# The second half of the differential values moved ahead of the products with the inverse, and score steps put in the places it leaves

## Chip, core and metric

The kernel runs on one core of a Trainium2 chip. The metric is the device time of one execution in microseconds (us). A core has a tensor engine (PE, with PEld for its weight loads), a vector engine (DVE), a scalar engine (ACT), GpSimd (POOL) and SyncE (SP), which here only issues transfers. Each engine works through its own list of instructions in order, and an instruction that waits holds up those behind it on its engine.

## What is computed

Two transformer blocks over 512 tokens of width 1024. The change is in the attention of the second block, which has two independent halves whose outputs are joined and multiplied by one output matrix:

```
# half 1: RWKV-7, 8 heads of 64, a recurrence over the tokens
sa = einsum('bhvk,bhk->bhv', state, -kk_t)
state = state * w_t + sa * (kk_t * a_t) + v_t * k_t
y_t = einsum('bhvk,bhk->bhv', state, r_t)
...
# half 2: differential attention, 4 heads, two score maps each
pr = softmax(where(dist >= 0, q k^T * scale - slopes * dist, NEG_INF))
attn = pr[:, :, 0] - lam * pr[:, :, 1]
out = einsum('bhqk,bhkv->bhqv', attn, vh)
```

The recurrence is done in 8 chunks of 64 tokens. Inside a chunk a triangular system has to be inverted. Products of fp32 values are made of three fp32r matmuls, from a value's high part and its rest (`whi`, `wlo` for weights, `xh`, `xl` for activations).

## The kernel before

All that follows is in `block2_attn`. First come the projections. For a weight chunk, a transfer brings `raw`, ACT casts it to `whi` (L168), and DVE or POOL subtracts to get `wlo` (L169). There are two buffers each of `whi` and `wlo`.

`inverse32` (L1642) inverts the diagonal 32x32 blocks on DVE alone, in a long chain of multiplies and sums, and ends with two transposes, `tN` (L1673) and `tT` (L1674). While it runs, PE does the last projections: the queries and keys of the differential half (`diff_qk`, tile `psd`), and its values (`diff_v`, L1288, tile `psdv`). `diff_v(0)` gives the first half of the values, `diff_v(1)`, called `values1`, the second half. Each is 96 matmuls over two weight chunks, whose `wlo` POOL makes. One step of `values1` is 12 matmuls.

Then the 64x64 inverses are put together. `psi` (L1443) multiplies `tN` with the blocks below the diagonal, in 32x32 matmuls; its result is copied to `pm`, half by DVE and half by ACT. A second product, also called `psi` (L1449), gives the corner, which is copied into `TT` (L1450). `chunk_in(0)` opens the bank `pxy` of chunk 0 (L1388, a product with the all-zero tile `zero`, and L1390). DVE copies it to `xs`, PE applies the inverse (`pu`, L1470), and the result `uv` goes into the new state (`pst`, L1480, tile `S`). The loop over the 8 chunks follows, each with `pxy`, `xs`, `pu`, `uv` and `pst` of its own.

The tile `zero` is written by POOL (L1352) into the space (tag `zq`) of `Qb`, a work tile of `inverse32`.

`diff_heads` is a generator, called `work`, of the softmax steps. A score step (16 of them, h a head, b a query block, of 128, 256, 384 or 512 keys) makes two products `z` on PE (L656), for each a sum with `dist` and a minimum on DVE (L657) and an exponential on ACT (L659), then on DVE a reciprocal (L662), a small product (L1722) and the difference of the two maps (L1723). A turned step transposes it (`t`, L675) and copies it to `w` (L677). A weighted step multiplies by the values (`o`, L683). Steps come in the order score 0, score 1, score 2, turned 0, score 3, turned 1, weighted 0, and so on.

The order on PE is written out by hand. `fill(n, of)` puts the next n steps of a generator at its place. `VF = (3, 2, 2, 2)` are the counts of the places before the loop and in chunk 0, `FILLS = (2, 2, 1, 6, 6, 0, 0)` those of the later chunks and of `tail`, which also puts all that is left. `rest()` runs what is left of `values1` and makes the tiles that take over the space of the activations `xh`: the states `S`, the second distance tile, and `yr`. DVE, ACT and POOL instructions are put in order by a scheduler.

Of the kernel before, what the change touches and what calls it, by code (L numbers as in the profile page):

```python
# [82 lines left out]
class Net:  # L83
# [999 lines left out]
    def block2_attn(self):  # L1083
        nc, A = self.nc, self.A
        v_, g_, s_, t_ = nc.vector, nc.gpsimd, nc.scalar, nc.tensor
        with ExitStack() as st:
# [192 lines left out]
            def diff_v(half):  # L1279
                pss = [p_.tile([128, 2, 256], F32, tag=n_, name="psdv") for p_, n_ in ((pz, "s"), (ptp, "t"))]  # L1280
                for c in range(2):
                    hi, lo = self.chunk(A["w_dv"][2 * half + c], g_)
                    for j in range(4):
                        k, cc = 4 * c + j, slice(j * 256, j * 256 + 256)
                        for t in range(4):
                            o, tb = pss[t // 2][:, t % 2, :], slice(t * 128, t * 128 + 128)
                            for i, (a, b) in enumerate(((xh, hi), (xh, lo), (xl, hi))):
                                t_.matmul(o, a[k][:, tb], b[:, cc], start=k == 0 and i == 0 and t % 2 == 0,  # L1288
                                          stop=k == 7 and i == 2, skip_group_check=True)
                        if k < 7:  # L1290
                            yield
                for t in range(4):
                    s_.activation(out=dv[:, t, half * 256:half * 256 + 256], in_=pss[t // 2][:, t % 2, :], func=AF.Copy, scale=rc[:, t:t + 1])
# [51 lines left out]
            values1 = diff_v(1)  # L1345
# [13 lines left out]
            def rest():  # L1359
                for _ in values1:  # L1360
                    pass
                dist2[1] = self.xp.tile([128, S], F32, tag="xh2", name="dist2")
                yr.extend(self.xp.tile([128, S], F32, tag=f"xh{4 + t}", name=f"yr{t}") for t in range(4))
                for i in range(2):
                    S2.append(self.xp.tile([128, 4, 2, 64], F32, tag=f"xh{i}", name=f"S{i}"))
                    g_.memset(S2[i], 0.0)
# [13 lines left out]
            fill = lambda n, of=work: [next(of, None) for _ in range(n)]  # L1380
            banks = {}

            def chunk_in(c):
                cp, par = c // 2, c % 2
                U, V = E[1 - par], E[par]
                p_, n_ = ((pr, "r"), (py, "y"))[c % 2]
                b = banks[c] = p_.tile([128, 512], F32, tag=n_, name="pxy")
                t_.matmul(b, zero[:, 0:128], zero, start=True, stop=False, skip_group_check=True)  # L1388
                for h in range(8):
                    t_.matmul(b[U, hs[h]], lm(par, cp, h)[V, 64 - 64 * par:128 - 64 * par], vt[V, cp, hs[h]], start=False, stop=True, skip_group_check=True)  # L1390
                s_.copy(out=uv2[V, c % 2, :], in_=vt[V, cp, :])
# [30 lines left out]
            with self.tc.manual_schedule(engines={mybir.EngineType.PE}):  # L1422

                TT = [pp.tile([128, 4, 2, 64], F32, tag=n_, name="TT") for n_ in ("pb0", "pb1", "e20", "e21")]
                pm = pp.tile([128, 4, 8, 32], F32, tag="bk2", name="pm")
                half = [(64 - 64 * par, slice(64 - 64 * par, 96 - 64 * par), slice(96 - 64 * par, 128 - 64 * par)) for par in range(2)]
                for t in range(4):
                    for _, lo, hi in half:
                        g_.memset(TT[t][hi, :, :, 0:32], 0.0)
                        v_.tensor_copy(out=TT[t][lo, :, :, 0:32], in_=tT[lo, :, 2 * t:2 * t + 2, :])  # L1430
                        s_.copy(out=TT[t][hi, :, :, 32:64], in_=tT[hi, :, 2 * t:2 * t + 2, :])

                def corner(ps, hh, rows, mm, out):
                    for par in range(2):
                        for cp in range(4):
                            for h in range(4):
                                mm(ps[half[par][rows], cp, h, :], par, cp, 4 * hh + h)
                    for par in range(2):
                        out(par, ps[half[par][rows]])

                for hh in range(2):
                    ps = ((pg, pv)[hh]).tile([128, 4, 4, 32], F32, tag="go"[hh], name="psi")
                    corner(ps, hh, 2, lambda o, par, cp, h: t_.matmul(o, lm(par, cp, h)[half[par][1], half[par][0] + 32:half[par][0] + 64],  # L1443
                                                                      tN[half[par][1], cp, h, :], start=True, stop=True),
                           lambda par, p: (s_.copy if par else v_.tensor_copy)(out=pm[half[par][2], :, 4 * hh:4 * hh + 4, :], in_=p))
                fill(VF[0], values1)
                for hh in range(2):
                    ps = pc.tile([128, 4, 4, 32], F32, tag="c", name="psi2")
                    corner(ps, hh, 1, lambda o, par, cp, h: t_.matmul(o, pm[half[par][2], cp, h, :], tT[half[par][2], cp, h, :], start=True, stop=True),  # L1449
                           lambda par, p: [(s_.copy if par else v_.tensor_copy)(out=TT[2 * hh + i][half[par][1], :, :, 32:64], in_=p[:, :, 2 * i:2 * i + 2, :])  # L1450
                                           for i in range(2)])
                chunk_in(0)
                fill(VF[1], values1)
                for c in range(8):
                    cp, par = c // 2, c % 2
                    U = E[1 - par]
                    b, uv, xs = banks[c], uv2[:, c % 2, :], xs2[:, c % 2, :]
                    if c:
                        for t in range(4):
                            t_.matmul(b[:, t * 128:t * 128 + 128], ar[t][:, c, :], S2[c % 2][:, t].rearrange("p e v -> p (e v)"),  # L1460
                                      start=False, stop=True, skip_group_check=True)
                    v_.tensor_copy(out=xs[U, 0:256], in_=b[U, 0:256])
                    v_.tensor_copy(out=xs[U, 256:512], in_=b[U, 256:512])
                    if c:
                        chunk_out(c - 1)
                    fill(FILLS[0]) if c else fill(VF[2], values1)
                    for g in range(2):
                        pu = pc.tile([128, 256], F32, tag="c", name="pu")
                        for h in range(4 * g, 4 * g + 4):
                            t_.matmul(pu[U, hs[h - 4 * g]], TT[h // 2][U, cp, h % 2, :], xs[U, hs[h]], start=True, stop=True)  # L1470
                        (s_.copy if g else v_.tensor_copy)(out=uv[U, 256 * g:256 * g + 256], in_=pu[U])
                    if c:
                        fill(FILLS[1])
                    else:
                        rest()
                        fill(VF[3])
                    if c < 7:
                        ps = pc.tile([128, 4, 64], F32, tag="c", name="pst")
                        for h in range(8):
                            t_.matmul(ps[E[h % 2], h // 2, :], bkt[:, c, hs[h]], uv[:, hs[h]], start=True, stop=True)  # L1480
                        for e in range(2):
                            new = S2[(c + 1) % 2][E[e], :, e, :]
                            if c == 0:
                                v_.tensor_copy(out=new, in_=ps[E[e]])
                            else:
                                old = S2[c % 2][E[e], :, e, :]
                                g_.tensor_tensor(out=new, in0=old, in1=dcs[E[e], :, c:c + 1].to_broadcast([64, 4, 64]), op=ALU.mult)
                                v_.tensor_tensor(out=new, in0=new, in1=ps[E[e]], op=ALU.add)
                    if c < 7:
                        chunk_in(c + 1)  # L1490
                    fill(FILLS[2])
                    if c in (4, 6):
                        norm_out(c // 2 - 2)
                if TAIL[0] == 0:
                    tail()
# [320 lines left out]
FILLS = (0, 2, 2, 4, 6)  # L1816
# [177 lines left out]
VF = (3, 2, 2, 2)  # L1994
# [18 lines left out]
FILLS = (2, 2, 1, 6, 6, 0, 0)  # L2013
# [33 lines left out]
```

## Time and profile before

| | us |
|---|---|
| median of 3 runs | 2049.07 (2044.24 to 2054.25) |
| profiled execution | 2044.56 |
| its span | 2042.8 |
| PE busy | 1931.4 |
| DVE busy | 1349.0 |
| ACT busy | 896.6 |
| POOL busy | 428.5 |

The profile describes one execution. Its span runs from the first to the last instruction; 1.76 us lie around it. The granted clock is the share of full speed that the tensor engine had: 1.00 is 2.4 GHz and 0.50 is 1.2 GHz. The stage that the change touches lies between 1470 and 1606 us of the span.

### The profile page before, as it was taken

What the parts mean: (1) busy time and instruction counts of PE and PEld (TensorE: products, weight loads), DVE (VectorE), ACT (ScalarE), POOL (GpSimd) and SP (SyncE); (2) the same over time, 40 slices, a digit from 0 to 9 for tenths busy, and PEclk for the clock granted to TensorE, in tenths of its full rate; (3) what the DMA queues carried; (4) which work ended last, traced back from release to release, by engine and by line L of the source; (5) the groups of instructions that cost most, each with busy time, mean ns of one, the idle gap of its engine ahead of it and who ended that gap; (6) DMA issues with size and microseconds to landing.
All of it is one profiled execution on the core that took longest, in us unless ns stands there. A gap on an engine that the chain in (4) does not pass through costs nothing. (4 is left out here: it accounts for less than half of the span.)

```text
span 2042.8 us, 29679 instructions
## 1 busy us (share of the span) xinstructions
PE 1931.4 (95%) x11652; PEld 1645.2 (81%) x11652; DVE 1349.0 (66%) x2286; ACT 896.6 (44%) x1538; POOL 428.5 (21%) x429
## 2 busy tenths in 40 slices
PE   9959998999999999988899999879989999999997
PEld 7736687999997877778899998768778788888886
DVE  6525668867777666557867676777858668666324
ACT  5425544434344455535434344534246545444321
POOL 2324310000001165420000001355333242111001
PEclk9979999999999999999999999889989999999998
DMA  4230042424222210114423232222210113322332
GB/s 160 70 69 20 28 143 77 133 75 136 70 93 91 85 43 27 35 55 145 142 75 111 86 106 61 97 88 68 73 53 27 66 57 102 100 96 93 94 94 70
DMA packets 57987, 169.38 MB, mean 83 GB/s; under 512 B 6288, under 2 KB 13368, under 8 KB 57848
## 3 DMA queue, kind: packets, MB, share of 16 engines
q1 hardware_dynamic: 54544, 162.51, 24.1%
q10 hardware_dynamic: 3224, 4.72, 1.2%
q8 instruction: 91, 1.49, 0.3%
q14 instruction: 48, 0.39, 0.1%
q0 software_dynamic: 80, 0.26, 0.0%
HBM read 161.70 MB, written 5.77 MB: 82 GB/s over the span
## 5 line engine op out<-in xcount | busy, mean ns | idle before, releaser
L168 ACT CAST whi<-raw 128x1024 fp32r<-128x1024 f32 (+3 forms) x146 | 144.4, 990 | 285.0 <-PE o L175 93.5
L169 DVE TENSOR_TENSOR wlo<-raw,whi 128x1024 fp32r<-128x1024 f32 (+3 forms) x138 | 163.9, 1188 | 127.3 <-ACT whi L168 126.8
L710 PE MATMUL pa<-t,h 128*128 128x256 f32 x960 | 177.3, 286 | 10.3 <-DVE u L884 8.4
L1018 POOL TENSOR_TENSOR acc<-acc,sqt 128x256 f32<-128x256 f32 (+1 forms) x58 | 70.5, 1215 | 487.7 <-ACT sqt L1017 485.8
L207 DVE TENSOR_TENSOR l<-r,h 128x1024 fp32r<-128x1024 f32 x104 | 127.0, 1221 | 53.8 <-ACT h L206 53.8
L710 PEld LDWEIGHTS pa<-t,h 128*128 128x128 f32 x960 | 152.1, 193 | 12.7 <-ACT ah L835 8.7
L710 PE MATMUL pa<-t,l 128*128 128x256 f32 x480 | 137.4, 286 | 1.9 <-DVE l L207 1.9
L206 ACT CAST h<-r 128x1024 fp32r<-128x1024 f32 x104 | 107.7, 1046 | 66.8 <-PE pd L175 20.6
L175 PE MATMUL o<-xl,whi 128*128 128x512 f32 (+1 forms) x352 | 134.6, 383 | 1.6 <-DVE xl L214 1.6
L174 PE MATMUL o<-xh,whi 128*128 128x512 f32 (+1 forms) x352 | 134.8, 383 | 0.0
L176 PE MATMUL o<-xh,wlo 128*128 128x512 f32 (+1 forms) x352 | 134.0, 381 | 0.0
L176 PE MATMUL pd<-ah,l 128*128 128x512 f32 x320 | 126.8, 396 | 2.0 <-DVE l L207 2.0
L174 PE MATMUL pd<-ah,h 128*128 128x512 f32 x320 | 126.7, 396 | 0.3 <-ACT h L206 0.3
L175 PE MATMUL pd<-al,h 128*128 128x512 f32 x320 | 126.6, 396 | 0.0
L710 PE MATMUL p<-t,h 128*128 128x256 f32 x640 | 117.8, 284 | 4.1 <-ACT h L206 4.1
L710 PE MATMUL pb<-t,h 128*128 128x256 f32 x640 | 115.9, 282 | 0.0
L710 PEld LDWEIGHTS p<-t,h 128*128 128x128 f32 x640 | 100.5, 191 | 6.0 <-ACT h L206 4.5
L710 PEld LDWEIGHTS pb<-t,h 128*128 128x128 f32 x640 | 99.8, 191 | 1.0
L206 ACT CAST h<-raw 128x768 fp32r<-128x768 f32 (+2 forms) x76 | 62.3, 820 | 84.9 <-PE pd L175 60.8
L710 PEld LDWEIGHTS pa<-t,l 128*128 128x128 f32 x480 | 93.0, 194 | 2.7 <-DVE l L207 2.7
L710 PE MATMUL p<-t,l 128*128 128x256 f32 x320 | 91.0, 284 | 3.0 <-DVE l L207 3.0
L710 PE MATMUL pb<-t,l 128*128 128x256 f32 x320 | 90.4, 283 | 1.1 <-DVE l L207 1.1
(548 smaller groups left out, 5337.1 us busy)
## 6 DMA issues: line engine op xcount, KB each, us to landing
r<-w_gu SPq DMA_DIRECT2D x88, 512.0 KB, 3.5
raw<-w_gu SPq DMA_DIRECT2D x56, 512.0 KB, 3.5
raw<-w_dn SPq DMA_DIRECT2D x48, 384.0 KB, 4.0
raw<-w_in SPq DMA_DIRECT2D x22, 512.0 KB, 3.5
raw<-w_dn SPq DMA_DIRECT2D x16, 448.0 KB, 3.2
raw<-w_qka SPq DMA_DIRECT2D x8, 512.0 KB, 3.7
raw<-w_dn SPq DMA_DIRECT2D x16, 256.0 KB, 2.6
raw<-w_out SPq DMA_DIRECT2D x8, 512.0 KB, 3.5
```

The lines of the kernel that those rows point to most:

```text
L168: nc.scalar.copy(out=hi[:, :n], in_=raw[:, :n])
L169: (eng or nc.vector).tensor_sub(out=lo[:, :n], in0=raw[:, :n], in1=f(hi[:, :n]))
L174: mm(out, lh, rh, start=start, stop=False)
L175: mm(out, lh, rl, start=False, stop=False)
L176: return mm(out, ll, rh, start=False, stop=stop)
L206: self.nc.scalar.copy(out=hi, in_=src)
L207: (eng or self.nc.vector).tensor_sub(out=lo, in0=src, in1=f(hi))
L710: self.nc.tensor.matmul(c, l, r, start=first and n == 0, stop=k == 3 and n == 2, skip_group_check=True)
L1018: return nc.gpsimd.tensor_add(out=self.acc[:, c], in0=self.acc[:, c], in1=t)
```

## The change

All of `values1` runs before `psi`, by a call of `rest()` there. The four fills that took steps of `values1` take steps of `work` now, three, two, two and two of them: score 0, 1 and 2 behind the first `psi`, turned 0 and score 3 behind `chunk_in(0)`, turned 1 and weighted 0 behind the copies to `xs`, score 4 and turned 2 behind `pu`. So nine steps of `work` less are left for the later places.

```diff
@@ -1438,19 +1438,20 @@
+                rest()
                 for hh in range(2):
                     ps = ((pg, pv)[hh]).tile([128, 4, 4, 32], F32, tag="go"[hh], name="psi")
...
-                fill(VF[0], values1)
+                fill(VF[0])
                 for hh in range(2):
                     ps = pc.tile([128, 4, 4, 32], F32, tag="c", name="psi2")
...
                 chunk_in(0)
-                fill(VF[1], values1)
+                fill(VF[1])
                 for c in range(8):
...
-                    fill(FILLS[0]) if c else fill(VF[2], values1)
+                    fill(FILLS[0]) if c else fill(VF[2])
...
                     if c:
                         fill(FILLS[1])
                     else:
-                        rest()
                         fill(VF[3])
```

On PE, before the change, 18 of the `psi` products stand between two products of the first half of the values; names are tiles, and `x18` counts equal neighbours.

```order
L1288 MATMUL psdv<-whi,xl_12090 128x256
L1288 MATMUL psdv<-whi,xh_12083 128x256
L1443 MATMUL psi<-tN,lms 32x32 x18
L1288 MATMUL psdv<-wlo,xh_12083 128x256
L1288 MATMUL psdv<-whi,xl_12091 128x256
```

After the change all 192 `psdv` stand ahead of `psi`, and PE has this behind the last of them, up to `pu` of chunk 0.

```order
L1288 MATMUL psdv<-whi,xl_12094 128x256
L1444 MATMUL psi<-tN,lms 32x32 x64
L656 MATMUL z<-dqk_13196,dqk_13197 128x128 x2
L656 MATMUL z<-dqk_13196,dqk_13197 128x256 x2
L656 MATMUL z<-dqk_13196,dqk_13197 128x384 x2
L1450 MATMUL psi_13993<-tT,pm 32x32 x32
L1450 MATMUL psi_14030<-tT,pm 32x32 x32
L1388 MATMUL pxy<-zero 128x512
L1390 MATMUL pxy<-vt,lms 64x64 x8
L675 MATMUL t<-ident,s 128x128
L656 MATMUL z<-dqk_13196,dqk_13197 128x512 x2
L675 MATMUL t<-ident,s 128x128 x2
```

The `psi` products are in one piece, and the places between them and `pu`, which held 36 and 48 `psdv`, hold scores and transposes; one `o` follows, then `pu`.

On DVE, after the change, the copies of the corner to `TT` and of the chunk to `xs` have the steps of scores 0 to 2 ahead of them; this is the end of those steps.

```order
L662 RECIPROCAL smst<-smst 128x1
L1722 SCALAR_TENSOR_TENSOR smst<-smst,c_12157,dsum 128x1
L657 ISA s,smst<-z,dist 128x384
L657 ISA smst 128x1
L1723 SCALAR_TENSOR_TENSOR s<-s,smst 128x256
L657 ISA s,smst<-z,dist 128x384
L657 ISA smst 128x1
L662 RECIPROCAL smst<-smst 128x1
L1722 SCALAR_TENSOR_TENSOR smst<-smst,c_12157,dsum 128x1
L1723 SCALAR_TENSOR_TENSOR s<-s,smst 128x384
L1451 COPY TT<-psi_13993 32x8x32 x2
L1451 COPY TT<-psi_14030 32x8x32 x2
```

Before, nothing stood between the copies to `pm` and those to `TT` on DVE.

On POOL, `zero` keeps its place after the change: ahead of the `wlo` of the second chunk of `diff_v(0)` (the first of `x2`) and of both chunks of `diff_v(1)`.

```order
L169 TENSOR_TENSOR wlo<-raw,whi 128x1024 x5
L1352 TENSOR_SCALAR zero<-ident 128x512
L169 TENSOR_TENSOR wlo<-raw,whi 128x1024 x2
L1366 MEMSET S_13873 128x512
L169 TENSOR_TENSOR wlo<-raw,whi 128x1024
L1366 MEMSET S_13875 128x512
```

Before, the three `wlo` behind `zero` stood together; now the clearing of a state stands ahead of the last.

## Rows read from the trace of the kernel before

**Rows 1.** The page: busy time of each engine, its share of the span, instructions.

```profile
PE 1931.4 (95%) x11652; PEld 1645.2 (81%) x11652; DVE 1349.0 (66%) x2286; ACT 896.6 (44%) x1538; POOL 428.5 (21%) x429
```

**Rows 2.** Busy time by stretch: length, then each engine, clock, DMA share, GB/s.

```profile
1519.77:1580.53 60.76, 59.25 (x648) 47.66 (x647) 53.45 (x190) 35.71 (x95) 22.12 (x24) 1.00 0.05 19
1580.53:1606.26 25.73, 23.20 (x150) 18.22 (x151) 21.85 (x91) 15.55 (x37) 5.66 (x4) 0.93 0.30 104
```

**Rows 3.** The chain that ended last, 1486 to 1518: start, length, work.

```profile
1486.32 1.94 PE psi L1443 x36
1488.25 6.97 PE psdv L1288 x47
...
1498.05 4.50 PE psdv L1288 x36
1502.55 3.86 PE psi L1449 x128
...
1507.91 7.44 PE psdv L1288 x48
1515.35 1.07 PE pu L1470 x16
1516.42 1.63 PE psdv L1288 x12
```

**Rows 4.** PE in order of time; in brackets the idle time before and its releaser.

```profile
1486.32 1.94 PE L1443 MATMUL psi<-tN,lms 32*32 32x32 f32 x36 [9.92 <-DVE tN L1673]
```

**Rows 5.** POOL in order of time, 1482 to 1495.

```profile
1482.65 1.49 POOL L1352 TENSOR_SCALAR zero<-ident 128x512 fp32r<-128x512 f32 x1 [13.76 <-DVE Pb L1668]
1484.11 2.37 POOL L169 TENSOR_TENSOR wlo<-raw,whi 128x1024 fp32r<-128x1024 f32 x1
1492.59 2.40 POOL L169 TENSOR_TENSOR wlo<-raw,whi 128x1024 fp32r<-128x1024 f32 x1 [6.12 <-ACT whi L168]
```

**Rows 6.** Stretches by granted clock, columns as in rows 2.

```profile
948.40:951.70 3.30, 3.30 (x18) 3.30 (x18) 2.62 (x4) 1.35 (x4) 0.00 (x0) 0.52 0.02 5
...
1486.30:1490.90 4.60, 4.58 (x49) 4.52 (x50) 4.06 (x9) 2.69 (x7) 0.17 (x1) 0.51 0.36 114
...
1507.95:1511.40 3.45, 3.45 (x17) 3.45 (x18) 0.77 (x2) 0.57 (x1) 0.66 (x1) 0.51 0.00 0
```

**Rows 7.** PE in order of time in the feed-forward part, as in rows 4.

```profile
946.51 0.50 PE L710 MATMUL p<-t,h 128*128 128x256 f32 x2 [2.07 <-ACT h L206]
947.77 0.39 PE L710 MATMUL p<-t,l 128*128 128x256 f32 x1 [0.76 <-DVE l L207]
```

**Rows 8.** DVE in order of time: copies of `psi`, a weight's rest.

```profile
1498.09 0.70 DVE L1445 COPY pm<-psi 32x512 f32<-32x512 f32 x1 [1.13 <-PE psi L1443]
...
1506.45 0.76 DVE L1450 COPY TT<-psi 32x256 f32<-32x256 f32 x2 [1.07 <-PE psi L1449]
...
1511.90 1.22 DVE L169 TENSOR_TENSOR wlo<-raw,whi 128x1024 fp32r<-128x1024 f32 x1 [3.19 <-ACT whi L168]
```

**Rows 9.** Score steps by source line: ns least/median/most, first and last start, forms.

```profile
L657 DVE CUSTOM_DVE_ANT_0 s<-z,dist x32: 278/486/691, 1518.5 to 1589.0; 128x128 f32<-128x128 f32 x8, 128x256 f32<-128x256 f32 x8, 128x384 f32<-128x384 f32 x8, 128x512 f32<-128x512 f32 x8
...
L659 ACT ACTIVATE s<-s,smst x32: 385/556/724, 1519.8 to 1589.7; 128x128 f32<-128x128 f32 x8, 128x256 f32<-128x256 f32 x8, 128x384 f32<-128x384 f32 x8, 128x512 f32<-128x512 f32 x8
L659 ACT ACTIVATION_READ_ACCUMULATOR s<-s,smst x32: 184/187/210, 1520.1 to 1590.4; 128x1 f32 x32
```

**Rows 10.** DVE groups by form, 1520 to 1606: count, busy us, mean ns, idle before.

```profile
L1722 DVE SCALAR_TENSOR_TENSOR smst<-smst,c,dsum 128x1 f32<-128x1 f32 x16 | 5.0, 319 | 0.2
...
L1723 DVE SCALAR_TENSOR_TENSOR s<-s,smst 128x384 f32<-128x384 f32 x4 | 3.6, 890 | 0.1
...
L662 DVE RECIPROCAL smst<-smst 128x1 f32<-128x1 f32 x16 | 2.4, 158 | 0.7 <-ACT s L659 0.5
```

**Rows 11.** PE in order of time: scores of 128 and of 512 keys.

```profile
1530.61 0.49 PE L656 MATMUL z<-dqk,dqk 64*128 64x128 f32 x4
...
1544.63 1.13 PE L656 MATMUL z<-dqk,dqk 64*128 64x512 f32 x4
```

## Prediction

> **What bounds the kernel now.** I read the page first. PE is busy for 95% of the span, DVE for 66% [rows 1], so time is mostly to be had where PE waits, or where it runs at half clock. Then the chain that ended last, in the stage of the change: from 1486.32 to 1518.05 us it is PE without a gap, `psi` and `psdv` in turns, up to `pu` and twelve more `psdv` [rows 3]. So here PE's work sets the pace, and the `psdv` stand where PE would otherwise wait for copies. Then PE in order of time: just ahead of this, it waits 9.92 us, put down to `tN` on DVE [rows 4]. Then POOL: `zero` waits 13.76 us for the last use of `Qb` in the inversion, ends at 1484.14, and the `wlo` behind it runs until 1486.48 [rows 5]. The `psdv` that PE wants next read this `wlo`. So two things end that wait at nearly the same time, `tN` and `wlo`. Last the windows: the 60.76 us of the loop hold 59.25 of PE at full clock and 53.45 of DVE; the 25.73 us behind it hold 23.20 of PE at a granted clock of 0.93, and DVE is busy for 21.85 [rows 2]. PE and DVE are both nearly full there.
>
> **The change, part by part.** The profiled execution took 2044.56 us, 4.5 us (0.2%) below the median of the three runs; I add up against the former and shift to the latter.
>
> *The long wait stays.* The moved `psdv` stand behind the ones that wait for `wlo`, and on POOL this `wlo` is still behind `zero`. PE starts at 1486.48 instead of 1486.32: +0.2. That nothing is gained here rests on the order alone, which the front shows for POOL.
>
> *The values in one piece.* At 1486.48, 47 `psdv` of the first half are left. PE ran at half clock from 1486.30 to 1490.90 [rows 6]. At the full-clock rate of 4.50 us for 36, 0.125 us each [rows 3], it does about 18 of the 47 until 1490.9 and the other 29 by 1494.5. The next chunk's `wlo` ends at 1494.99 [rows 5]; the 92 `psi` covered this before, now PE waits: +0.5 to +1, I take +0.7. The 96 `psdv` took 4.50 + 7.44 + 1.63 = 13.57 us before [rows 3], as part of the 48 ran at half clock (1507.95 to 1511.40 [rows 6]). In one piece at 0.125 they take 12.0: -1.6.
>
> *From `psi` to `pu`.* Before, 1515.35 - 1498.05 = 17.30 us, of which 11.94 are `psdv` (36 and 48): 5.36 us of other PE work [rows 3]. Now this and four scores: 0.49 us of PE for 128 keys and 1.13 for 512 [rows 11], on a line between them 0.70 and 0.92, plus some 0.7 for the transposes and `o`: 9.3 us. But DVE has a chain to do in this order. From the end of `psi`: the copy to `pm` 0.70 and a `wlo` of 1.22 [rows 8] end at 1.9. Score 0: two reads of `z` at 0.28 and the second exponential of 0.39 + 0.19 [rows 9], reciprocal and product 0.16 + 0.32 [rows 10]: 3.5. Score 1, with reads of 0.42 and an exponential of 0.50 + 0.19 (on a line between least and most): 5.5. Score 2 with 0.55 and 0.61 + 0.19: 7.9. The differences L1723, 0.89 for 384 keys [rows 10] and in proportion 0.3 and 0.6: 9.7. Only then come the copies to `TT`, 2 x 0.76 [rows 8]: 11.2; `xs` and `w` add about 1.2: 12.4. On PE the third score waits for the reads of the second (4.7), ends at 5.2, and the second `psi` (3.86), `pxy` (1.50, from 1506.41 to 1507.91), `t`, `z` and `o` (1.8) end at 12.4 too [rows 3]. So `pu` comes 12.4 us behind `psi`, with 9.3 of work: +3.1 of waiting. Bounds: 0 if the reads come sooner (ACT and DVE overlap more), 5 if each hand-over costs more than these rows show.
>
> *The clock in that stretch.* The trace has no such stretch, so I take bounds. In the feed-forward part PE waited 2.07 and 0.76 us within 2 us [rows 7], and ran at a granted 0.52 from 948.40 to 951.70 [rows 6]: 1.2 GHz. Here it waits 3.1 us within 5, after 3.9 us of 32x32 products; and before the change the clock fell at 1507.95 after 32x32 products with no wait at all [rows 3, 6]. So I take it that the clock falls. At half clock 36 `psi` took 1.94, at full 128 took 3.86 [rows 3]: a factor of 1.8. The second `psi` then costs 6.9 instead of 3.86, `pxy` 2.7 instead of 1.5, the last `z`, `t` and `o` 3.2 instead of 1.8: +5.6, of which some overlaps the start of the fall. I take +5. The lower bound is 0: in the loop, waits of 60.76 - 59.25 = 1.5 us in all left the clock at 1.00 [rows 2].
>
> The Trainium skill, page "TensorE: Matmul & The Clock Gate", section "A second HAM failure mode: psum-queue depth-cycling", tells of a kernel whose PE paused briefly between groups of matmuls while it cycled through PSUM banks, and whose clock swung between its two levels. Here `z` has two banks that DVE must read before the next score. By that page the term is +5, by the loop's row 0; rows 6 and 7 side with the page.
>
> *Behind `pu`.* Nine steps fewer are left behind. The loop's places hold as many steps as before, and its PE and DVE are as full, so I expect its length unchanged. Behind the loop, PE waited 2.5 us, and a clock of 0.93 over 25.73 us means 3.6 at half speed, worth 1.8 [rows 2]: 4.3 us at most. DVE has less to do there now, but the last chunk's norm, over DVE, ACT and POOL, still follows `chunk_out(7)`. I take half: -2, between 0 and -4.3.
>
> Sum: 0.2 + 0.7 - 1.6 + 3.1 + 5.0 - 2.0 = +5.4 us. That is 2050.0 for the profiled execution, and 2054.5 beside the median of 2049.07 (+0.26%).
>
> **The rivals.** *The clock holds* (0 instead of +5): 2049.5. For it speaks the loop at 1.00; against it rows 6 and 7. *The values fill the long wait.* If `wlo` came sooner, 9.92 us would go, and with them the half clock up to 1490.90, worth 2.3: 5.4 - 12.2 = -6.8, or 2042.3, faster by 0.3%. Against it stands POOL's order. *The clock stays down into the loop*, the one that makes it clearly slower: a chunk of the loop is 60.76 / 7 = 8.7 us, nearly all PE; at 1.8 times as long it costs up to 6.6 more each. One chunk gives 2061, two give 2068. It decides from 0.7 of a chunk on, where the total passes +10. Each half-clock stretch of rows 6 ended within 5 us, under dense products; these are smaller. *The tail takes it all back*, with the clock held: 5.4 - 5 - 2.3 = -1.9, or 2047.2.
>
> **How the numbers follow.** Forecast 0.60; clock holds 0.18; tail takes it back 0.05; values fill the wait 0.04; clock down into the loop 0.13. A difference of 0.5%, 10.2 us, is about what a measurement of this kernel can tell from no change. Only the slow rival passes it, with a little of the forecast's upper end: slower 0.15. Faster by 10 us would need the filled wait and the tail together: 0.03. The rest, 0.82, is within. The range leaves out the filled wait and the second chunk at half clock: 2045 to 2062.
>
> **What would show it.** Right: PE idle for about 10 us up to 1486.5, then 143 `psdv` with a wait of some 0.7 us at 1494 to 1495; `psi` ending near 1511; three waits of `z` on DVE; the copies to `TT` over 8 us behind `psi`; a granted clock of 0.50 during the second `psi`; `pu` some 18 us behind the first. Wrong: `psdv` running between 1477 and 1486; or a granted 1.00 between `psi` and `pu`; or a tail shorter by more than 4 us, where I have under-rated what DVE's lighter end is worth; or 0.50 beyond the state of chunk 1.

## The result, and the profile after

The changed kernel takes 2060.84 us (median of 7 executions, 2057.96 to 2064.84), the kernel before 2049.07 (2041.79 to 2054.25): a ratio of 1.0065, interval 1.0047 to 1.0083. It is slower by 0.65%; the forecast was +0.26%. The profiled execution of the changed kernel took 2062.12 us, 17.6 more than that of before, so the two profiles overstate the difference of the medians (11.8) by some 6 us.

PE's line of the page after, which answers to [rows 1], shows PE busy for 13.5 us more with the same 11652 products:

```profile
PE 1944.9 (94%) x11652; PEld 1655.5 (80%) x11652; DVE 1349.6 (66%) x2286; ACT 897.4 (44%) x1538; POOL 426.0 (21%) x429
```

So the products are slower, not more. Where, the windows tell. First the stage from the last normalisation ahead of the inverse to the first `psg`, a product behind the loop and its tail, of before:

```profile
1411.50:1601.60 190.10, 176.11 (x1573) 149.45 (x1572) 145.07 (x382) 81.48 (x181) 66.01 (x58) 0.96 0.17 56
```

And the same stage after, followed by `psi` to `pu`, the stretch at half clock, the loop and the tail (the last two answer to [rows 2]), and a second stretch at half clock inside the loop:

```profile
1412.40:1620.70 208.30, 190.96 (x1587) 160.05 (x1586) 150.38 (x398) 83.00 (x182) 65.11 (x58) 0.89 0.16 52
1511.43:1530.20 18.77, 16.50 (x167) 11.83 (x167) 9.90 (x32) 5.54 (x18) 2.04 (x2) 0.52 0.09 29
1512.65:1539.70 27.05, 25.59 (x229) 19.76 (x230) 13.54 (x48) 8.00 (x27) 4.76 (x5) 0.50 0.07 21
1533.65:1602.48 68.83, 66.95 (x665) 54.86 (x665) 51.55 (x197) 35.18 (x89) 20.60 (x23) 0.91 0.03 11
1556.84:1563.50 6.66, 6.66 (x39) 6.08 (x39) 3.61 (x21) 2.08 (x6) 0.86 (x1) 0.50 0.01 2
1602.48:1624.20 21.72, 19.25 (x125) 14.89 (x124) 18.84 (x65) 11.60 (x25) 4.91 (x4) 0.92 0.34 117
```

The stage is 18.2 us longer. PE's idle time in it goes from 14.0 (190.10 - 176.11) to 17.3 us: +3.3. The other 14.9 are PE busy for longer, at a granted clock of 0.89 instead of 0.96. Not all of that is the clock: the window after holds 14 products more (1587 for 1573), which before come behind its end. With the same products, over the whole execution, it is the 13.5 us of the page. A clock of 0.50 is 1.2 GHz, 1.00 is 2.4, so the means stand for about 15 us at half clock before (2 x 0.04 x 190) and 46 after (2 x 0.11 x 208). The 31 more would cost at most about 15, if every product took twice as long. One stretch of 27.05 us holds most of them, and it runs on through `pu` into chunk 1; the loop, at 1.00 before, is at 0.91.

POOL in order of time after, which answers to [rows 5], and below it PE, which answers to [rows 4]; the brackets name idle time and releaser:

```profile
1483.50 1.49 POOL L1352 TENSOR_SCALAR zero<-ident 128x512 fp32r<-128x512 f32 x1 [13.77 <-DVE Pb L1668]
1484.95 2.36 POOL L169 TENSOR_TENSOR wlo<-raw,whi 128x1024 fp32r<-128x1024 f32 x1
1493.46 2.39 POOL L169 TENSOR_TENSOR wlo<-raw,whi 128x1024 fp32r<-128x1024 f32 x1 [6.14 <-ACT whi L168]
```

```profile
1487.37 0.58 PE L1288 MATMUL psdv<-wlo,xh 128*128 128x256 f32 x1 [10.13 <-POOL wlo L169]
...
1495.90 0.39 PE L1288 MATMUL psdv<-wlo,xh 128*128 128x256 f32 x1 [0.58 <-POOL wlo L169]
...
1507.49 3.93 PE L1444 MATMUL psi<-tN,lms 32*32 32x32 f32 x128
1511.35 0.49 PE L656 MATMUL z<-dqk,dqk 64*128 64x128 f32 x4
1513.80 1.43 PE L656 MATMUL z<-dqk,dqk 64*128 64x256 f32 x4 [1.96 <-DVE smst L657]
1515.54 2.25 PE L656 MATMUL z<-dqk,dqk 64*128 64x384 f32 x4 [0.32 <-DVE smst L657]
1517.72 6.47 PE L1450 MATMUL psi<-tT,pm 32*32 32x32 f32 x128
...
1530.20 0.58 PE L1471 MATMUL pu<-xs,TT 64*64 64x64 f32 x3
```

The long wait is still there, 10.13 us, now put down to `wlo`. Behind the first `psi` PE waits twice for DVE, 2.28 us together. The clock fell in the first of these waits (a granted 0.62 from 1511.84 to 1513.80); the second `psi`, 4 us behind the wait, takes 6.47 us where the first takes 3.93. From 1515.54 to `pu` PE does not wait again. It is DVE that waits for PE there, before both copies to `TT`:

```profile
1521.18 0.76 DVE L1451 COPY TT<-psi 32x256 f32<-32x256 f32 x2 [0.62 <-PE psi L1450]
1524.23 0.76 DVE L1451 COPY TT<-psi 32x256 f32<-32x256 f32 x2 [2.28 <-PE psi L1450]
```

### The profile page after: what moved, and what is told of

The parts are those of the page before. It is cut to its first block, busy times and chain, and to the rows that moved or that the text cites. A ratio compares the mean times of both kernels' runs of the same rounds, so it can differ in the third digit from the quotient of the medians.

```text
span 2060.4 us, 29680 instructions
## 1 busy us (share of the span) xinstructions
PE 1944.9 (94%) x11652; PEld 1655.5 (80%) x11652; DVE 1349.6 (66%) x2286; ACT 897.4 (44%) x1538; POOL 426.0 (21%) x429
```

## The experiments

Three questions. Is the loss the clock (theory 1) or the waits between `psi` and `pu` (theory 2)? What keeps the values out of the long wait (theory 3)? And can both be had? Dense products are here the `psdv` and the added ones, weights of 128x128 against 256 or 512 columns. Each kernel was timed in turns with the kernel before on one chip; the ratios are to that.

### Dense products behind `psi`, and no scores behind `psi`

Two kernels that part theory 1 from 2. The first adds eight products whose result nobody reads (`vt` by the identity):

```diff
+                def warm(n, p_, n_):
+                    b = p_.tile([128, 512], F32, tag=n_, name="warm")
+                    for _ in range(n):
+                        t_.matmul(b, self.ident, vt[:, 0, :], start=True, stop=True)
...
                 for hh in range(2):
+                    if hh:
+                        warm(2, pr, "r")
                     ps = ((pg, pv)[hh]).tile(... name="psi")
...
-                fill(VF[0])
+                for n in (2, 1, 1):
+                    fill(1)
+                    warm(n, pr, "r")
                 for hh in range(2):
+                    if hh:
+                        warm(2, pr, "r")
                     ps = pc.tile(... name="psi2")
```

> The changed kernel with eight dense products added (vt by the identity, 128x512, result not read): two between the halves of psi, two behind score step z128, one each behind z256 and z384, two between the halves of psi2. They cost about 0.9 us each at the full clock, some 7 us together, of which 2 to 3 us may lie in PE's own waits (1.96 us ahead of z256, 0.32 ahead of z384). Theory 1 (the loss is the granted clock: about 46 us at half clock between the inverse and the first out product, against 13 before): the half clock behind psi goes or shrinks to under 10 us, 8 to 13 us come back, 5 are paid: 2050 to 2055 us. Theory 2 (the loss is the order and the waits of DVE and ACT between psi and pu, clock aside): the dummies only add, 2064 to 2068 us.

The second takes the three score steps between `psi` and `psi2` away; they follow later:

```diff
-VF = (3, 2, 2, 2)
+VF = (0, 2, 2, 2)
```

> The changed kernel with no score step between psi and psi2 (the three go to the later places). Theory 2 (waits): DVE and ACT come to the copies of pm and TT about 3 us sooner, pu starts 3 to 5 us sooner behind psi, and 3 us or more come back: 2056 to 2058 us. Theory 1 (clock): psi, psi2 and the 64x64 products stand back to back with still less dense work among them, the clock falls to 0.5 behind psi as in the changed kernel and stays down into chunk 1; pu may start sooner, but what is gained is under 2 us: 2059 to 2063 us.

With the dummies 2053.11 us, ratio 1.0024 (1.0012 to 1.0035); without the scores 2059.41, ratio 1.0059 (1.0044 to 1.0075), which is not told apart from the changed kernel. The windows of the kernel with dummies: its stage, `psi` and what follows, then the 27.05 us that were at 0.50, then the loop.

```profile
1411.40:1612.00 200.60, 185.83 (x1604) 152.45 (x1603) 150.47 (x398) 82.76 (x182) 65.17 (x58) 0.96 0.17 54
1506.48:1525.00 18.52, 18.52 (x289) 11.88 (x289) 8.57 (x28) 7.01 (x20) 0.40 (x1) 1.00 0.09 30
1512.65:1539.70 27.05, 27.00 (x313) 18.11 (x311) 17.22 (x61) 11.38 (x36) 4.77 (x5) 1.00 0.03 11
1525.50:1600.00 74.50, 72.56 (x766) 58.66 (x765) 62.32 (x227) 43.13 (x110) 25.46 (x28) 1.00 0.10 30
```

The windows of the kernel without the scores: `psi` and the start of `psi2`, then the stretch at half clock.

```profile
1506.00:1512.60 6.60, 6.60 (x202) 6.47 (x201) 2.62 (x3) 3.49 (x7) 0.00 (x0) 0.91 0.02 6
...
1511.30:1536.00 24.70, 23.93 (x206) 17.97 (x202) 13.34 (x42) 7.54 (x23) 4.73 (x5) 0.52 0.07 23
```

Eight products, about 0.99 us each, were added, and the kernel became 7.7 us faster than the changed one (8.4 by the two ratios, since the kernel before varied between the series): the clock stays at 1.00 from `psi` to the end of the loop, and from the first `psi` product to `pu` it takes less time with the dummies (1506.5 to 1527.8, 21.3 us) than without (1507.5 to 1530.2, 22.7). Without scores the clock falls all the same, at 1511.30, while PE is busy for the whole 6.60 us of the window. In the changed kernel the fall lay in a wait, which the dummies fill too; but here no wait is needed for it. From 1506.44 until the clock falls PE does the 32x32 products of `psi` and `psi2`, with nothing dense beside them. Theory 1 holds. Theory 2 expected 2064 to 2068 and 2056 to 2058.

### Part of the values back behind `psi`

This undoes a part of the change: 36 of the 96 products return to their place of before. They stand there instead of the three score steps, which follow later as in the run without scores.

```diff
-                rest()
+                fill(5, values1)
                 for hh in range(2):
                     ps = ((pg, pv)[hh]).tile(... name="psi")
...
-                fill(VF[0])
+                rest()
```

> The changed kernel with 36 of the 96 products back between psi and psi2, in place of the three score steps there (which go later); 60 stay in front of psi. Theory 1 (what is missing behind psi is dense work): the clock stays full through psi2 and falls later or for a shorter time, 2051 to 2057. Theory 2 (it is the score steps in the waits, on DVE and ACT): with none of them between psi and psi2 it gains what the run without them there gained, 1 to 2 us, 2058 to 2060.

It takes 2053.89 us, ratio 1.0038 (1.0025 to 1.0051). Its windows: from `psi` to `psi2`, then the half clock.

```profile
1500.56:1513.00 12.44, 12.44 (x294) 12.19 (x293) 4.32 (x6) 4.28 (x9) 0.00 (x0) 1.00 0.15 46
1513.00:1527.00 14.00, 13.22 (x70) 7.99 (x69) 8.12 (x32) 5.67 (x18) 2.04 (x2) 0.51 0.13 39
```

With 36 `psdv` between them both `psi` run at 1.00; the clock falls behind the second, where the changed kernel has small products too, and for 14 us instead of 27. This is theory 1 with the kernel's own work in place of dummies. PE has no wait between `psi` and the fall in this run or in the one without scores; the two differ in the place of the 36 products.

### What holds the long wait open

The changed kernel with `zero` in a buffer that is free early, so that POOL goes on to `wlo` without waiting for the inverse:

```diff
-            zero = pp.tile([128, S], F32R, tag="zq", name="zero")
+            zero = self.sm.tile([128, S], F32R, tag="rkv", name="zero", bufs=1)
```

> The changed kernel with the zero tile in a buffer that is free early, so that POOL's zero does not stand ahead of the chunk's wlo cast. Theory 3a (zero alone holds the long wait in front of the values): the wlo casts come some 8 us sooner, the values fill the wait, psi starts at about 1497 instead of 1507.6, and with the clock loss unchanged the time is about 2051. Theory 3b (zero is one of two: ACT's copies of tT into TT stand ahead of the whi cast of the last chunk): about 47 of the 96 products run ahead of tN in the wait, but the last 48 start where they do now, psi starts within 1 us of 1507.6, and the time is 2059 to 2063.

The same, with `rest()` ahead of the copies of `tT` and ACT's half of these copies on DVE:

```diff
+                rest()
                 for t in range(4):
                     for _, lo, hi in half:
...
-                        s_.copy(out=TT[t][hi, :, :, 32:64], in_=tT[hi, :, 2 * t:2 * t + 2, :])
+                        v_.tensor_copy(out=TT[t][hi, :, :, 32:64], in_=tT[hi, :, 2 * t:2 * t + 2, :])
```

> As the run before (zero early), and the values stand ahead of the copies of tT into TT in the order of the program, with the ones that ACT had on DVE, so that neither cast waits for the inverse. Theory 3b: all 96 products run in the long wait ahead of tN, and psi starts at about 1495 instead of 1507.6. Theory 1 beside it (the loss behind psi is the clock, and no dense work is left there): the half clock of 27 us stays behind psi, so the gain is the 12 us of the start and no more: 2047 to 2051 us. If the wait is only moved (tT and TT come late to psi2 and pu), 2056 or more.

They take 2065.08 us (1.0085, 1.0066 to 1.0105) and 2062.05 (1.0071, 1.0057 to 1.0086): no gain. The first is far from theory 3a (2051) and 2 us above the range of 3b, the second missed its expectation of 2047 to 2051 by 11. With `zero` early, in PE's and ACT's order of time (this execution came to the stage 4.6 us later than that of the changed kernel):

```profile
1499.73 0.58 PE L1288 MATMUL psdv<-whi,xh 128*128 128x256 f32 x1 [12.30 <-ACT whi L168]
...
1502.15 0.58 PE L1288 MATMUL psdv<-wlo,xh 128*128 128x256 f32 x1 [1.84 <-POOL wlo L169]
```

```profile
1495.31 3.30 ACT L1431 COPY TT<-tT 32x256 f32<-32x256 f32 x8 [18.71 <-DVE tT L1674]
1498.63 1.04 ACT L168 CAST whi<-raw 128x1024 fp32r<-128x1024 f32 x1
```

PE does the first half of the values to its end and then waits as long as ever, for a `whi` that stands on ACT behind the copies of `tT`. With those on DVE, ACT and PE read:

```profile
1490.54 1.24 ACT L1391 COPY uv<-vt 64x512 f32<-64x512 f32 x2 [18.74 <-DVE tT L1674]
1491.81 1.04 ACT L168 CAST whi<-raw 128x1024 fp32r<-128x1024 f32 x1
```

```profile
1492.91 0.58 PE L1288 MATMUL psdv<-whi,xh 128*128 128x256 f32 x1 [10.25 <-ACT whi L168]
```

Next in line were the two copies of `vt` to `uv`, which ACT holds until the inverse is done. So theory 3b had the mechanism, a cast behind something that waits for the inverse, but one more of them than I had listed. With these copies on DVE too:

```diff
-                s_.copy(out=uv2[V, c % 2, :], in_=vt[V, cp, :])
+                (s_.copy if c > 1 else v_.tensor_copy)(out=uv2[V, c % 2, :], in_=vt[V, cp, :])
```

> The run with the values ahead of the copies of tT showed why psi still started at 1508.4: half 0 was done at 1482.7, but the next whi cast stood on ACT behind the uv copies of chunks 0 and 1, which wait for tT, and PE waited 10.25 us for it. Here these two copies go to DVE as well, so that nothing on ACT ahead of the casts waits for the inverse. Theory 3c (the queues of ACT and POOL, not the place of the values, keep the long wait empty): the 96 products of the second half run from about 1483 to 1495, psi starts at 1494 to 1496 instead of 1507.6, and with the half clock behind it unchanged the time is 2047 to 2051. Rival (the casts of POOL slow the inverse on DVE, or the products wait for something else): psi not before 1503, 2056 or more.

It takes 2049.11 us, ratio 1.0015 (1.0002 to 1.0027): 11.7 us under the changed kernel, or about 10 by the two ratios. Its windows: the stage, and the half clock behind `psi`, which starts at 1493.9 now.

```profile
1411.00:1608.70 197.70, 190.87 (x1587) 159.02 (x1586) 157.38 (x408) 78.82 (x172) 65.50 (x57) 0.90 0.17 56
1497.10:1527.75 30.65, 28.64 (x258) 21.91 (x254) 16.70 (x52) 9.05 (x28) 4.77 (x5) 0.50 0.11 36
```

PE's idle time in the stage falls from 17.3 us to 6.8; its busy time is that of the changed kernel to 0.1 us. The waits are gone and the clock's loss stays, as theories 3c and 1 had it.

### Both together

The same kernel with the eight dense products of the first experiment (unread again):

> The run before with the eight dense products between psi and psi2 of the first experiment (result not read). Theory 1 with 3c: both gains add, the clock holds behind psi, and the time is 7 to 9 us under that of the run before, 2039 to 2043: faster than the kernel before. Rival (with the wait filled the clock holds without help, since PE comes to psi without an idle gap): the dummies cost 2 to 5 us, 2050 or more.

2044.05 us, ratio 0.9993 (0.9981 to 1.0006): not told apart from the kernel before. The stage's window:

```profile
1413.40:1603.20 189.80, 185.35 (x1604) 151.34 (x1603) 157.41 (x408) 78.56 (x172) 65.54 (x57) 0.98 0.18 58
```

The clock is at 0.98 and PE idles for 4.5 us. The gain over the run without dummies is 5.1 us, less than the 7 to 9 expected. In the profiles the stage gains 7.9 us (197.70 to 189.80), as much as in the first pair (208.30 to 200.60); why the medians show less stays open. The rival (clock holds without help) is out.

The kernel before with the same freed queues, and its own values spread: 36 products in the long wait, 12 behind `psi`, 24 behind `psi2`, 12 more ahead of `pu`, and 12 behind it.

```diff
                 for t in range(4):
                     for _, lo, hi in half:
 ...
+                fill(3, values1)
 ...
-VF = (3, 2, 2, 2)
+VF = (1, 2, 1, 2)
```

> The kernel before the change (no score step in the small waits) with the same freeing of the queues: zero early, the copies of tT and the two uv copies on DVE, and 36 of the 96 products in the long wait, 12 between psi and psi2, 36 between psi2 and pu, 12 behind pu. Theory 1 with 3c: the dense products behind psi hold the clock as before, the long wait goes, psi ends at about 1491.5 instead of 1498.05 and pu starts at about 1504 instead of 1515.3: 2037 to 2041. Rival (what is saved ahead of psi comes back as a wait for pm, TT or S in the loop): 2045 to 2049.

2042.28 us, ratio 0.9979 (0.9965 to 0.9993). PE ahead of `psi`, and the windows of the stage, of the stretch at half clock and of what follows:

```profile
1483.16 1.00 PE L1444 MATMUL psi<-tN,lms 32*32 32x32 f32 x26 [3.18 <-DVE tN L1674]
```

```profile
1404.70:1592.00 187.30, 179.76 (x1573) 152.51 (x1572) 151.78 (x392) 77.12 (x171) 66.20 (x57) 0.95 0.18 59
1484.00:1505.00 21.00, 21.00 (x286) 20.09 (x283) 11.13 (x28) 3.45 (x7) 2.04 (x2) 0.51 0.11 36
1505.00:1592.00 87.00, 82.86 (x832) 66.94 (x832) 72.49 (x273) 50.92 (x130) 27.78 (x28) 1.00 0.14 47
```

The profiled execution took 2034.14 us, the shortest of the twelve. Idle time is halved against before (7.5 us for 14.0), but the clock falls at 1484, behind the wait and early in `psi`. The 12 products between `psi` and `psi2` do not bring it back; it comes back at 1505, among the 24 behind `psi2`. PE is busy for 3.7 us longer than before (179.76 for 176.11), and the time is 1.3 us above the range of the expectation. Three tries to get it back: three unread products in the wait of 3.18 us; these and two more inside each `psi`; and real work, with five steps of the values ahead of `psi` and one in each later place.

```diff
+                warm(3)
                 for hh in range(2):
                     ps = ((pg, pv)[hh]).tile(... name="psi")
```

> The split run showed half clock from 1484 to 1505, from a wait of 3.18 us for tN ahead of psi on through psi and psi2. Here three dense products (vt by the identity, result not read) stand in that wait, where PE does nothing anyway: they cost at most 0.3 us. Theory 1a (the idle wait brings the clock down): the clock holds through psi, and most of the 10 us that the half clock cost there come back: 2033 to 2037 us. Theory 1b (the 32x32 products themselves bring it down): it falls all the same within psi or psi2, some 5 to 10 us later than now, and 2 to 4 us come back: 2038 to 2041.

```diff
                 for hh in range(2):
+                    if hh:
+                        warm(2)
                     ps = ...   # psi, and the same for psi2
```

> As the run before, and two more dense products between the halves of psi and two between those of psi2, which cost some 3.6 us on PE where nothing hides them. Theory 1b: now the clock holds through psi and psi2, 8 to 10 us come back and 3.6 are paid: 2035 to 2038 us. Theory 1a: they only cost, 3 us above the run before.

```diff
-                fill(3, values1)
+                fill(5, values1)
...
-VF = (1, 2, 1, 2)
+VF = (1, 1, 1, 2)
```

> The split run with the real work of the values in the wait in place of dummies: 60 products ahead of tN, 12 between psi and psi2, 12 between psi2 and pu in each of its two places. The wait of 3.18 us goes to under 0.5. Theory 1a: the clock holds through psi and falls later, behind psi2, where dense work is now missing, 2036 to 2040 us. Theory 1b: it falls in psi or psi2 and stays down through the 64x64 products for some 20 us as in the changed kernel, 2041 to 2046.

They take 2043.69 us (0.9980, 0.9970 to 0.9990), 2042.21 (0.9972, 0.9959 to 0.9986) and 2042.83 (0.9986, 0.9975 to 0.9998): not told apart from one another or from the split run. The three in windows and PE's order (the first kernel's half clock and wait, the second's windows ahead of the fall and behind it, the third's half clock and wait):

```profile
1493.00:1511.00 18.00, 16.31 (x194) 15.36 (x191) 8.65 (x22) 3.45 (x7) 2.04 (x2) 0.53 0.10 31
```

```profile
1497.78 0.42 PE L1456 MATMUL psi<-tT,pm 32*32 32x32 f32 x4 [1.69 <-DVE pm L1452]
```

```profile
1492.39:1502.60 10.21, 9.68 (x208) 8.15 (x208) 8.46 (x21) 1.97 (x3) 0.38 (x1) 1.00 0.12 45
1503.40:1517.00 13.60, 13.60 (x109) 11.15 (x108) 2.97 (x7) 1.25 (x4) 2.04 (x2) 0.50 0.13 40
```

```profile
1492.00:1510.00 18.00, 15.08 (x176) 14.17 (x176) 8.17 (x20) 2.40 (x6) 2.04 (x2) 0.53 0.10 30
```

```profile
1497.53 0.68 PE L1450 MATMUL psi<-tT,pm 32*32 32x32 f32 x9 [2.92 <-DVE pm L1446]
```

Filling the wait ahead of `psi` only puts the fall off until `psi` has run (theory 1b), and a new wait opens ahead of `psi2`, for `pm`, which DVE copies behind the now sixteen copies of `tT` and the two of `vt`. With dummies inside each `psi` the clock holds through the first, as 1b has it, and then falls among the two dummies inside `psi2` and stays down for 13.6 us. So 1b was missed there, and in size in the first run too, and dense products among small ones did not hold the clock everywhere; why not there stays open. The best versions beat the kernel before by 0.2 to 0.3%.

## Why the prediction was wrong

The time lay inside the range, but the change was taken to be within 0.5% and is slower by 0.65%. Of the signs that were named for being wrong one came, a granted 0.50 beyond the state of chunk 1 (`pst`, from 1533.65). By the prediction's steps, on the profiled executions:

- *The long wait stays* (+0.2): right. 10.13 us for 9.92, for the reason named, `wlo` behind `zero`. Later runs showed that it was one of three locks: ACT's copies of `tT` and of `vt` held the next cast just as well. The rival "values fill the long wait" could not have come true by `zero` alone.
- *The values in one piece* (wait +0.7, gain -1.6): right. The wait was 0.58, and 95 products took 11.65 us on the chain that ended last, the view of [rows 3], so -1.8:

```profile
1495.90 11.65 PE psdv L1288 x95
```

- *From `psi` to `pu`* (+3.1 of waiting): 2.28 measured, but elsewhere. The prediction had DVE's chain up to the copies to `TT` set `pu`; it came in time, and DVE waited for PE there. The 2.28 are PE's waits ahead of two scores. Over the stage PE's idle time grew by 3.3 for the 4.0 forecast in all waits.
- *The clock in that stretch* (+5): **this step failed, by size.** That the clock falls was right, the second `psi` ran at half clock as named, and `pu` came 18.8 us behind `psi` where some 18 were named. Up to `pu` PE was busy for 16.50 us, where 9.3 of work and the +5 make 14.3. But the term was summed only up to `pu`, as if the clock came back there. It came back at 1539.70, 9.5 us later, and fell again from 1556.84 to 1563.50. In all the clock cost about 15 us in the profile for the 5 forecast: the 13.5 us by which PE is busy for longer, and the 1.8 that the values gave back. Scaled by the medians (11.8 of 17.6 us) this would be nearer to 10; which part of the 6 us between belongs to the clock stays open, since only one execution was profiled.
- The rival *the clock stays down into the loop* is what happened. It priced one chunk at 6.6 us, 2061 in all, and had a chance of 0.13. In the loop the clock cost 5.4 us (below). That 2061 is so near to the 2060.84 measured is in part luck: between the profiles the difference is 17.6 us, not 12. Its counter-argument was that each half-clock stretch of [rows 6] ended within 5 us. Dense `psdv` or feed-forward products followed each of them, and behind `psi` the change takes away just these. That they ended those stretches is argued; the split run, at half clock for 21 us with 12 of them inside and 24 behind `psi2`, shows that a few need not end one. The rows that resembled the new place most, 32x32 products without a wait ahead of the fall at 1507.95, were read for whether the clock falls, not for how long it stays down without dense work.
- *Behind `pu`* (-2, with the loop unchanged): nothing was gained, and the loop is 8.1 us longer (60.76 to 68.83). With the dummies, at a clock of 1.00, the same 665 products of the loop take 63.41 us:

```profile
1529.76:1593.17 63.41, 61.47 (x665) 49.81 (x664) 52.23 (x199) 35.61 (x91) 21.10 (x24) 1.00 0.04 12
```

So 2.65 of the 8.1 us are 17 products more than before (648), where the tail has 25 fewer, and 5.4 are the clock. The tail is 4.0 us shorter (25.73 to 21.72), but that is the moved work: PE's busy time there fell from 23.20 to 19.25, while its idle time stayed (2.53 and 2.47) and the clock too (0.93 and 0.92) [rows 2].

The prediction weighed a section of the Trainium skill, "A second HAM failure mode: psum-queue depth-cycling" in "TensorE: Matmul & The Clock Gate", where brief pauses of PE between groups go with a swinging clock. It gave the right sign here, and in the changed kernel the clock did fall in a pause. But the run without scores speaks against that cause: no pause, PE busy for 6.60 of 6.60 us, and the clock fell.

Forecast with the measured sizes in place: 0.2 + 0.6 - 1.8 + 2.3 + 15 - 0 = about +16 of the 17.6 that the two profiles differ by. What made the loss is shown by the dummies and by the 36 products put back. How long the clock stays down is only observed, not explained: 14 us with the 36 products back, 27 in the changed kernel and 31 with the values early, all with no dense products behind `psi2`, but also 14 to 21 us in the split runs, which have some.

## What to carry to other kernels

Work that fills a wait can have a second use: dense products among small ones kept TensorE at 2.4 GHz in most of these runs, and moving them away cost more than the order gained. Before moving dense work, read what PE is left with there, and price the half clock beyond the end of the stretch: here it lasted 9.5 us past `pu` and came a second time. When work is moved ahead into a wait, follow its inputs back on every engine: POOL's queue held one instruction and ACT's two groups of copies that waited for the same late result, and the gain came only when all three were out of the way.

## What was not expected of the hardware

- PE can be busy without a gap and still lose its clock: 6.60 us of 6.60, all but the first 0.4 in 32x32 products, granted 0.91, then 0.52 for 24.70 us. Adding about 8 us of unread 128x512 products made the kernel 7.7 us faster.
- POOL's `wlo` slows DVE while both run. In the run with `zero` early the multiplication of 128x512 took 2.84 us, started beside a `wlo` of POOL, in the changed kernel 1.10 alone. It ended at 1480.05, 0.97 us behind the end of this `wlo` (1479.08): nearly all of its own work came after. So casts moved into the inverse delay `tN`, which starts 42.8 us behind the first multiplication of the inverse (L1656) instead of 41.0. The Trainium skill, "SBUF — State Buffer", section "SBUF: two separate sides", has a VectorE operation with two SBUF inputs and a GpSimd operation that reads SBUF share a pair of ports, which the one that starts first holds for its whole instruction; the rows below agree. In DVE's and POOL's order of time, of the run with `zero` early:

```profile
1477.21 2.84 DVE L1662 TENSOR_TENSOR Pb<-Xb,Lb 128x512 f32<-128x512 f32 x1
```

```profile
1476.67 2.41 POOL L169 TENSOR_TENSOR wlo<-raw,whi 128x1024 fp32r<-128x1024 f32 x1 [2.41 <-ACT whi L168]
```

and of the changed kernel:

```profile
1472.67 1.10 DVE L1662 TENSOR_TENSOR Pb<-Xb,Lb 128x512 f32<-128x512 f32 x1
```
